# Attention by pairs of heads in a two-layer trunk on one NeuronCore: row halves for the logits, column halves for the products with V

## The chip, the core and the metric

The kernel runs on one core of a Trainium2 chip. A core has a matrix engine (TensorE, PE in the rows below, with its weight loads as PEld), a vector engine (DVE), a scalar engine (ACT), GpSimd (POOL) and SyncE (SP), which issues the loads of the weights. The metric is the time of one execution on the device in microseconds; the number given is the median of three runs.

## What is computed

A trunk of two residual layers over 256 tokens of width 1024, batch 1, float32. Each layer is attention, then a SwiGLU feed-forward of width 2816. Cut to what the change touches:

```python
# layer 0: 8 FoX heads (softmax with forget gates) and 8 stick-breaking heads, 64 wide
# layer 1: 8 MoBA heads (64 wide, bias on the logits) and 8 MLA heads (q and k 96 wide, v 64 wide)
logits = jnp.einsum("bhqd,bhkd->bhqk", qb, k) * scale     # per head, causal
p = weights_of(logits)                                    # softmax, or stick-breaking products
out = jnp.einsum("bhqk,bhkd->bhqd", p, v)                 # per head, 64 columns
x = x + concat(out of all 16 heads) @ w_out
x = x + swiglu(rms_norm(x))
```

With 256 tokens every query block sees at most two key blocks of 128, so a head has three 128 x 128 blocks of logits: one for the first 128 queries, two for the rest.

## The kernel before

Every large product (projections, output projection, feed-forward) is exact in three passes: each operand is split into two float32r parts, and `mm3` issues high by high, high by low and low by high into an accumulator `acc`. ACT makes the high part of a weight piece (`whi<-raw`), DVE the low part (`wlo<-raw,whi`). The attention itself uses plain float32 products (`mm` on float32), which the trace shows as two records each, and its tiles in PSUM are called `ps`; there are four of these.

A group is four heads; layer 0 has the groups Fox 0, Fox 1, Stick 2, Stick 3, layer 1 has Moba 0, Mla 2, Moba 1, Mla 3. For one head the steps on TensorE are:

- **Logits** (`products`, L615): two products into one `ps` tile, 128 columns for the first query block, 256 for the second. For FoX, MoBA and stick-breaking heads q and k are 64 rows: an even head lies in partitions 0 to 63, an odd one in 64 to 127 (operands `fT`, `sbT`). For MLA heads they are 96 rows (`mT`).
- DVE and ACT make the weights from them (`score`, L660 and L1065): for softmax a masked minimum on DVE (`lg`), two exponentials on ACT (`pm`), a reciprocal and two scalings on DVE.
- **Transposes** (`transp`, L624): three 128 x 128 transposes of the weights (`ident,pm` or `ident,w`), and a copy by ACT into `wt`.
- **Products with V** (`values`, L635): two products, of 256 and of 128 columns, into the group's tile `O`. The tile of V for a head is 128 columns wide, with the head's 64 columns in one half and zeros in the other (`v_zeros`, L584), so that two heads add into the same 128 partitions.

`heads_loop` (L728) writes the order by hand: the logits of head i, filler, the transposes of head i-1, filler, the products of head i-1 with V, filler. Filler are the large products that are due next (projections of later groups, parts of the output projection). How much is pulled in is told by an estimate of TensorE's time, `fl.clk`, which `mm` (L330) and `tr` advance; work of the other engines is put off with `fl.at` to a later value of that clock. The scheduler of the tile framework then moves steps marked `urgent` forward on each engine, so the final order is read from the built program and not from the loop.

Of the kernel before, what the change touches and what calls it, by code (L numbers as in the profile page):

```python
# [98 lines left out]
class Ordered:  # L99
    """An engine that keeps the order of emission while on is set, and puts nothing later before what it kept."""  # L100
# [19 lines left out]
class Weights:  # L120
    """Weights in the order of their use: loads ahead, then the exact split in two float32r parts."""
# [12 lines left out]
    def add_load(self, src, row0, total, kts, col0, ncols, beside=None):  # L134
        """beside: the load whose tile has room for this one too."""
# [11 lines left out]
    def cut(self, u, pieces):  # L147
        """pieces: (load, its rows and columns, the place of them in the unit)."""
# [15 lines left out]
    def add_first(self, src, total, col0, ncols, extra0, extra):  # L164
        """two units of half the rows, with a few more columns from another place; loads of two row tiles."""
# [90 lines left out]
def trunk_kernel(ctx: ExitStack, tc: tile.TileContext, x, ffn_norm, w_gate_up, w_down, rel_bias,  # L256
# [60 lines left out]
    def rsqrt(v, n, o=None):  # L317
        """v ** -0.5 by logarithm and exponential, with a Newton step."""
# [11 lines left out]
    def mm(o, a, b, start, stop):  # L330
# [4 lines left out]
        fl.clk += max(n / 2.4 + 2.5, 107) if b.dtype == R32 else 4 * (n / 2.4 + 1)  # L335
# [126 lines left out]
    # gains: rows of 128, transposed to columns  # L462
# [21 lines left out]
    class XT:  # L484
# [8 lines left out]
        def transposes(self, q):  # L493
            """tiles 2q and 2q+1 of the features."""
# [75 lines left out]
    def featT(src, gain):  # L570
        """[tok, 2, 256] token-major -> [128, 2 pairs, 256 tok]."""
# [12 lines left out]
    def v_zeros():  # L584
        """the tiles of V, for the two groups at hand: a head's columns are in the left or the right half."""
        res = []
        for i in range(2):
            t = att.tile([P, 2, 4, P], F32, name=nm("V"), bufs=1)
            for h in range(4):
                pool.memset(t[:, :, h, 64 - h % 2 * 64:128 - h % 2 * 64], 0.0)  # L590
            res.append(t)
        return res
# [4 lines left out]
    def v_rows(V, src, scale):  # L597
        """src: [tok, 4, 64] of the two row tiles."""
        for tok in range(2):
            for i in range(2):  # L600
                act.activation(V[:, tok, i::2, i * 64:i * 64 + 64], src[tok][:, i::2], AF.Identity,
                               scale=1.0 if scale is None else scale[:, tok:tok + 1])
        return V

    class Group:
        """four heads; score(h) gives the weights' tile, prep() brings q and k in place."""
# [28 lines left out]
        def values(self, h):  # L635
# [22 lines left out]
    class Softmax(Group):  # L658
        @urgent
        def score(self, h):  # L660
            s = self.products(h)
# [3 lines left out]
            pm = att.tile([P, 384], F32, name=nm("pm"), tag="pm")  # L665
# [5 lines left out]
            def exps():  # L671
# [3 lines left out]
                               accum_out=l[:, 1:2])  # L675

# [10 lines left out]
        def normed(self, pq, pk, rs, r2, gain):  # L687
            """q and k of a group of 64-wide heads, as their products end: squares, factors, scaled rows."""
# [39 lines left out]
    def heads_loop(groups, lead):  # L728
        """a head's scores, then the products of the head before it, filler in between."""
        n, tail = 4 * len(groups), 4500  # L730
# [3 lines left out]
        for i in range(n + 1):  # L734
            b = max(fl.total - tail - fl.used, 0) / (n - i) if i < n else tail
            if i < n:
                g, h = groups[i // 4], i % 4
# [702 lines left out]
```

## Time and profile before

| | |
|---|---|
| three runs | 635.42, 635.65, 635.81 us; median 635.65 us |
| span of the profiled execution, first to last instruction | 633.6 us |
| TensorE busy | 626.0 us, 99% |
| VectorE busy | 427.5 us, 67% |
| ScalarE busy | 339.8 us, 54% |
| attention of layer 0 | about 39 to 131 us of the span |
| feed-forward of layer 0, first projections of layer 1 | about 131 to 358 us |
| attention of layer 1 | about 358 to 433 us |
| feed-forward of layer 1 | about 433 us to the end |

The profiled execution is not one of the three timed runs, and only its span is known: the median lies 2.0 us above it, for what comes before the first and after the last instruction. A record of a product on TensorE lasts longer than the time until the next one starts, since products overlap in the array; what a product costs is therefore read from one start to the next.

### The profile page before, as it was taken

The numbers are of one execution on the slowest core, as the hardware profiler recorded it, in microseconds if no ns is written. First come the engines' busy times: TensorE is split into PE (matmuls) and PEld (weight loads), VectorE is DVE, ScalarE is ACT, GpSimd is POOL, SyncE is SP. The second block draws the span as 40 slices with busy tenths as digits, with TensorE's granted clock in tenths as the row PEclk, the third lists the DMA queues.
The fourth block names the chain that finished last, engine by engine and source line by source line (L and its number), as shares of the span: only waits on it lengthen the run. The fifth ranks groups of instructions, "written<-read, shape, count | busy, mean of one in ns | idle before, by whom it ended". The sixth has DMA issues, their size and how long they took to land.

```text
span 633.6 us, 11099 instructions
## 1 busy us (share of the span) xinstructions
PE 626.0 (99%) x4370; PEld 575.3 (91%) x4370; DVE 427.5 (67%) x915; ACT 339.8 (54%) x731; POOL 22.6 (4%) x66
## 2 busy tenths in 40 slices
PE   8999999999999999999999999999999999999997
PEld 7888998779999999988889989788999999998897
DVE  4897766666876777745556697896687677774541
ACT  6865565563544455444447585976554445454430
POOL 8300000000000000000010000000000000000000
PEclk9999999999999999999999999999999999999999
DMA  8955234446664563744556325263266456375500
GB/s 262 338 179 184 96 121 134 133 133 212 205 222 162 181 218 135 232 162 171 169 181 208 116 84 199 67 200 121 93 202 226 158 184 214 135 233 166 200 34 33
DMA packets 84212, 106.19 MB, mean 168 GB/s; under 512 B 3532, under 2 KB 69394, under 8 KB 84032
## 3 DMA queue, kind: packets, MB, share of 16 engines
q1 hardware_dynamic: 82880, 101.49, 49.5%
q0 software_dynamic: 1120, 3.86, 1.9%
q8 instruction: 34, 0.56, 0.4%
q10 hardware_dynamic: 160, 0.14, 0.1%
q14 instruction: 18, 0.15, 0.1%
HBM read 104.41 MB, written 3.17 MB: 170 GB/s over the span
## 4 chain that ended last, share of the span: by engine, by line
PE 92%; DVE 3%; DMA 2%; ACT 2%; SPq 1%; issue 0%; ACTq 0%
PE acc L113 80%; PE ps L113 11%; DVE wlo L113 1%; DMA raw<-in_ev_w_in 1%; DMA x<-in_x 1%; DVE sm L113 1%; ACT whi L113 1%; ACT V L113 0%; SPq L404 0%; SPq L205 0%; DVE qkn L113 0%; ACT fT L113 0%; DVE lg L113 0%; DVE m L113 0%; ACT sqh L113 0%
## 5 line engine op out<-in xcount | busy, mean ns | idle before, releaser
L113 DVE TENSOR_TENSOR wlo<-raw,whi 128x512 fp32r<-128x512 f32 (+3 forms) x300 | 241.5, 828 | 85.8 <-ACT whi L113 85.0
L113 ACT ACTIVATE whi<-raw 128x512 fp32r<-128x512 f32 (+3 forms) x300 | 209.3, 740 | 129.9 <-PE acc L113 117.5
L113 PE MATMUL acc<-xh,whi 128*128 128x256 f32 x768 | 218.6, 285 | 0.0
L113 PE MATMUL acc<-xh,wlo 128*128 128x256 f32 x768 | 217.4, 283 | 0.0
L113 PE MATMUL acc<-xl,whi 128*128 128x256 f32 x768 | 217.4, 283 | 0.0
L113 PEld LDWEIGHTS acc<-xh,whi 128*128 128x128 f32 x768 | 147.4, 192 | 0.4 <-issue 0.3
L113 PEld LDWEIGHTS acc<-xl,whi 128*128 128x128 f32 x768 | 147.4, 192 | 0.0
L113 PEld LDWEIGHTS acc<-xh,wlo 128*128 128x128 f32 x768 | 147.3, 192 | 0.0
L113 PE MATMUL acc<-whi,hl 128*128 128x512 f32 (+1 forms) x198 | 73.3, 370 | 0.0
L113 PE MATMUL acc<-whi,hh 128*128 128x512 f32 (+1 forms) x198 | 73.2, 370 | 0.0
L113 PE MATMUL acc<-wlo,hh 128*128 128x512 f32 (+1 forms) x198 | 73.1, 369 | 0.0
L113 PE MATMUL acc<-whi,xh 128*128 128x256 f32 (+2 forms) x240 | 71.6, 298 | 0.0
L113 PE MATMUL acc<-whi,xl 128*128 128x256 f32 (+2 forms) x240 | 69.3, 289 | 0.0
L113 PE MATMUL acc<-wlo,xh 128*128 128x256 f32 (+2 forms) x240 | 69.2, 288 | 0.0
L113 DVE TENSOR_TENSOR gs<-acc,rbc 128x512 f32<-128x512 f32 x44 | 30.4, 691 | 37.4 <-PE acc L113 37.3
L113 ACT ACTIVATE hh<-t 128x256 fp32r<-128x256 f32 x44 | 18.4, 418 | 69.4 <-DVE t L113 69.4
L113 PEld LDWEIGHTS acc<-whi,xl 128*128 128x128 f32 x240 | 45.7, 190 | 0.7 <-issue 0.7
L113 PEld LDWEIGHTS acc<-wlo,xh 128*128 128x128 f32 x240 | 45.9, 191 | 0.1
L113 PEld LDWEIGHTS acc<-whi,xh 128*128 128x128 f32 x240 | 45.8, 191 | 0.2
L113 PEld LDWEIGHTS acc<-wlo,hh 128*128 128x128 f32 x198 | 37.3, 188 | 6.7
L113 PEld LDWEIGHTS acc<-whi,hh 128*128 128x128 f32 x198 | 37.3, 188 | 6.7
L113 PEld LDWEIGHTS acc<-whi,hl 128*128 128x128 f32 x198 | 37.3, 188 | 6.7
(179 smaller groups left out, 682.1 us busy)
## 6 DMA issues: line engine op xcount, KB each, us to landing
raw<-in_ffn_w_gate_up SPq DMA_DIRECT2D x44, 1024.0 KB, 5.5
raw<-in_ffn_w_down SPq DMA_DIRECT2D x20, 1024.0 KB, 5.0
raw<-in_ev_w_in SPq DMA_DIRECT2D x10, 1024.0 KB, 8.2
raw<-in_od_w_in SPq DMA_DIRECT2D x6, 1024.0 KB, 5.5
raw<-in_ev_w_out SPq DMA_DIRECT2D x4, 1024.0 KB, 4.8
raw<-in_od_w_out SPq DMA_DIRECT2D x4, 1024.0 KB, 5.5
brep<-bd POOLq DMA_DIRECT2D x1, 2048.0 KB, 8.6
raw<-in_ffn_w_down SPq DMA_DIRECT2D x4, 512.0 KB, 3.3
```

The costliest lines, as they stand in the source:

```text
L113: r = f(*a, **k)
```

## The change

Heads are taken two at a time.

- `scores(pr)` issues the logits of an even and an odd head of 64 rows alternately: both first query blocks, then both second ones. The even head is in the upper row half of the array, the odd head in the lower. For MLA, whose heads have 96 rows, the order is the same, with no halves.
- `values(pr)` uses V tiles of 64 columns without zeros. The even head writes partitions 0 to 63 of `O`, the odd head 64 to 127, so their products lie in the two column halves of the array; they alternate too. `v_tiles` takes the place of `v_zeros`, and `v_rows` needs one ACT instruction for each row tile where it had two.
- `heads_loop` goes by pairs: 8 steps for four groups where it had 16, with two heads' transposes together, other shares of filler, and a longer reserve at the end (`tail`). Flags "e" keep a pair's logits behind the exponentials of the pair before.
- The tiles `pm` and `m` get four buffers, and FoX makes two masks ahead.
- The clock of `mm` counts 120 ns at least for a float32r product (107 before) and half the time for products that are meant to lie beside each other.

```diff
-    def mm(o, a, b, start, stop):
+    def mm(o, a, b, start, stop, beside=1):
...
-        fl.clk += max(n / 2.4 + 2.5, 107) if b.dtype == R32 else 4 * (n / 2.4 + 1)
+        fl.clk += max(n / 2.4 + 15, 120) if b.dtype == R32 else 4 * (n / 2.4 + 1) / beside
...
-            t = att.tile([P, 2, 4, P], F32, name=nm("V"), bufs=1)
...
+        return [att.tile([P, 2, 4, 64], F32, name=nm("V"), bufs=1) for _ in range(2)]
...
-            for i in range(2):
-                act.activation(V[:, tok, i::2, i * 64:i * 64 + 64], src[tok][:, i::2], AF.Identity,
-                               scale=1.0 if scale is None else scale[:, tok:tok + 1])
+            act.activation(V[:, tok], src[tok], AF.Identity, scale=1.0 if scale is None else scale[:, tok:tok + 1])
...
-        def products(self, h):
-            qT, kT = self.heads[h]
-            s = ps()
-            mm(s[:, 0:P], qT[:, 0:P], kT[:, 0:P], True, True)
-            mm(s[:, P:384], qT[:, P:256], kT, True, True)
-            return s
+        def scores(self, pr):
+            two = [(self.heads[2 * pr + i], ps()) for i in range(2)]
+            n = 2 if self.heads[0][0].shape[0] == 64 else 1
+            for (qT, kT), s in two:
+                mm(s[:, 0:P], qT[:, 0:P], kT[:, 0:P], True, True, n)
+            for (qT, kT), s in two:
+                mm(s[:, P:384], qT[:, P:256], kT, True, True, n)
+            for i, (_, s) in enumerate(two):
+                self.score(2 * pr + i, s)
...
-            wt = self.wt[h]
-            o = self.O[:, h // 2 * 256:h // 2 * 256 + 256]
-            mm(o, self.V[:, 0, h], wt[:, 0:256], h == 0, False)
-            mm(o[:, P:256], self.V[:, 1, h], wt[:, 256:384], False, h == 3)
+            o = self.O[:, pr * 256:pr * 256 + 256]
+            for b in range(2):
+                for i in range(2):
+                    wt = self.wt[2 * pr + i][:, b * 256:384 - (1 - b) * P]
+                    mm(o[64 * i:64 * i + 64, b * P:256], self.V[:, b, 2 * pr + i], wt, b == 0, b == 1, 2)
...
-        n, tail = 4 * len(groups), 4500
+        n, tail = 2 * len(groups), 6000
...
+                if i > 0:
+                    g.ready(pr, "e")
+                g, pr = groups[i // 2], i % 2
+                g.scores(pr)
+            fl.pull((0.35 if i < n else 0.6) * b)
...
+                for j in range(2):
+                    g1.transp(2 * pr1 + j)
```

On TensorE in layer 0, first group, third head, the program before reads as follows: the logits of the third head (`ps_791`) stand between the two products of the first head with V (`ps_780`), with float32r products (`acc`) on both sides.

```order
L113 MATMUL acc_691<-wlo_479,xh_257 128x256
L113 MATMUL acc_691<-whi_478,xl_261 128x256
L113 MATMUL ps_780<-wt_761,V_353 128x256
L113 MATMUL ps_791<-fT_644,fT_637 128x128
L113 MATMUL ps_791<-fT_644,fT_637 128x256
L113 MATMUL ps_780<-wt_761,V_353 128x128
L113 MATMUL acc_691<-wlo_479,xh_263 128x256
```

The program of the change at its first products with V, again on TensorE (`ps_929` is the group's `O`, `ps_960` and `ps_961` are the logits of the next pair):

```order
L113 MATMUL acc_922<-xl_187,whi_707 128x256
L113 MATMUL acc_922<-xh_179,wlo_708 128x256
L113 MATMUL ps_929<-wt_846,V_353 64x256
L113 MATMUL ps_929<-wt_852,V_353 64x256
L113 MATMUL ps_929<-wt_846,V_353 64x128
L113 MATMUL ps_929<-wt_852,V_353 64x128
L113 MATMUL ps_960<-fT_904,fT_897 128x128
L113 MATMUL ps_961<-fT_904,fT_897 128x128
L113 MATMUL ps_960<-fT_904,fT_897 128x256
L113 MATMUL ps_961<-fT_904,fT_897 128x256
L113 MATMUL acc_922<-xh_189,whi_707 128x256
```

Where one head's two products stood, four products of two heads stand, 64 partitions of output each; the pair's logits follow in one block. In the whole program the logits of 64 rows stand in 22 places before (20 with one head, 2 with two) and in 10 after (8 with one pair, 2 with two pairs one behind the other), the products with V in 32 and in 16.

The second place is TensorE at the end of layer 1's attention: the last head's transposes (`ps_5257`), its products with V (`ps_5168`), and the output projection. Before:

```order
L113 MATMUL ps_5257<-ident,pm_5218 128x128 x3
L113 MATMUL acc_4957<-whi_4970,oh_5128 128x512
L113 MATMUL acc_4957<-wlo_4971,oh_5128 128x512
L113 MATMUL acc_4957<-whi_4970,ol_5132 128x512
L113 MATMUL ps_5168<-wt_5261,V_3861 128x256
L113 MATMUL ps_5168<-wt_5261,V_3861 128x128
L113 MATMUL acc_4956<-whi_4970,oh_5130 128x512
```

And in the change, where `pm_5135` and `pm_5142` are the last two heads and `ps_5167` is their `O`:

```order
L113 MATMUL ps_5198<-ident,pm_5135 128x128 x2
L113 MATMUL ps_5204<-ident,pm_5142 128x128 x3
L113 MATMUL acc_4949<-whi_4969,ol_5115 128x512
L113 MATMUL ps_5167<-wt_5202,V_3841 64x256
L113 MATMUL ps_5167<-wt_5208,V_3841 64x256
L113 MATMUL ps_5167<-wt_5202,V_3841 64x128
L113 MATMUL ps_5167<-wt_5208,V_3841 64x128
L113 MATMUL acc_4950<-whi_4969,oh_5111 128x512
```

Between the last transposes and the products that need their copies stood three products of 512 columns; now one stands there. The pair before the last has the same row of steps.

## Rows read from the trace of the kernel before

**Rows 1.** The page: busy time of each engine, share of the span, instructions.

```profile
PE 626.0 (99%) x4370; PEld 575.3 (91%) x4370; DVE 427.5 (67%) x915; ACT 339.8 (54%) x731; POOL 22.6 (4%) x66
```

**Rows 2.** The page: the chain that ended last, share of the span by engine.

```profile
PE 92%; DVE 3%; DMA 2%; ACT 2%; SPq 1%; issue 0%; ACTq 0%
```

**Rows 3.** TensorE's groups by shape: operands, count | busy us, mean ns.

```profile
L113 PE MATMUL ps<-wt,V 128*128 128x256 f32 x64 | 19.8, 390 | 0.0
...
L113 PE MATMUL ps<-fT,fT 64*128 64x256 f32 x32 | 8.4, 377 | 0.0
...
L113 PE MATMUL ps<-sbT,sbT 64*128 64x256 f32 x16 | 4.8, 377 | 0.0
```

**Rows 4.** Timeline of TensorE (start, duration, records): logits among transposes, transposes alone.

```profile
62.10 0.27 PE L113 MATMUL ps<-ident,pm 128*128 128x128 f32 x1
62.30 0.92 PE L113 MATMUL ps<-fT,fT 64*128 64x128 f32 x4
63.15 0.44 PE L113 MATMUL ps<-ident,pm 128*128 128x128 f32 x2
...
63.55 0.28 PE L113 MATMUL acc<-xl,whi 128*128 128x256 f32 x1
...
68.38 0.49 PE L113 MATMUL ps<-ident,pm 128*128 128x128 f32 x3
...
68.83 0.28 PE L113 MATMUL acc<-xl,whi 128*128 128x256 f32 x1
```

**Rows 5.** Timeline of TensorE: logits of two heads, one behind the other.

```profile
38.73 0.28 PE L113 MATMUL acc<-wlo,xh 128*128 128x256 f32 x1
38.93 0.93 PE L113 MATMUL ps<-fT,fT 64*128 64x128 f32 x8
39.80 0.38 PE L113 MATMUL acc<-whi,xl 128*128 128x256 f32 x1
40.02 0.28 PE L113 MATMUL acc<-whi,xh 128*128 128x256 f32 x1
```

**Rows 6.** Timeline of TensorE: one head's products with V between filler.

```profile
64.73 0.28 PE L113 MATMUL acc<-xh,wlo 128*128 128x256 f32 x1
64.85 0.81 PE L113 MATMUL ps<-wt,V 128*128 128x256 f32 x4
...
65.62 0.28 PE L113 MATMUL acc<-xl,whi 128*128 128x256 f32 x1
```

**Rows 7.** Timeline of TensorE: transposes with 8 columns of output (forget gates).

```profile
27.67 0.38 PE L113 MATMUL ps<-ident,fg 128*8 128x128 f32 x2 [1.24 <-DVE sm L113]
27.81 0.37 PE L113 MATMUL acc<-whi,xh 128*128 128x256 f32 x1
28.01 0.28 PE L113 MATMUL acc<-wlo,xh 128*128 128x256 f32 x1
```

**Rows 8.** Timeline of weight loads: the first behind rows 7, and behind rows 5.

```profile
27.78 0.19 PEld L113 LDWEIGHTS acc<-whi,xh 128*128 128x128 f32 x1
...
39.80 0.19 PEld L113 LDWEIGHTS acc<-whi,xl 128*128 128x128 f32 x1 [0.33 <-issue]
```

**Rows 9.** Windows: stretch, its length, busy us of each engine, clock, DMA share, GB/s.

```profile
39.00:58.00 19.00, 18.77 (x143) 16.65 (x142) 16.21 (x62) 12.21 (x38) 0.00 (x0) 1.00 0.50 162
...
358.00:433.00 75.00, 74.80 (x471) 63.36 (x471) 60.70 (x213) 56.39 (x165) 0.00 (x0) 1.00 0.35 117
```

**Rows 10.** ACT's groups by shape in 360 to 440 us: the copy of transposed weights.

```profile
L113 ACT ACTIVATE wt<-ps 128x384 f32<-128x384 f32 x16 | 7.9, 492 | 9.3 <-PE ps L113 9.3
```

**Rows 11.** Timeline of TensorE at the end of layer 1's attention: last transposes, last V.

```profile
430.94 0.49 PE L113 MATMUL ps<-ident,pm 128*128 128x128 f32 x3
431.18 0.48 PE L113 MATMUL acc<-whi,oh 128*128 128x512 f32 x1
...
432.07 0.92 PE L113 MATMUL ps<-wt,V 128*128 128x256 f32 x4
```

More of the change, by code (lines that the diff above doesn't have):

```diff
@@ L582, in featT, with v_tiles @@
         return t
-    def v_zeros():
-        res = []
-        for i in range(2):
-            t = att.tile([P, 2, 4, P], F32, name=nm("V"), bufs=1)
[L589 to L592, printed above, removed]
+    def v_tiles():
+        return [att.tile([P, 2, 4, 64], F32, name=nm("V"), bufs=1) for _ in range(2)]
     def heads_of(a):
@@ L599, in v_rows @@
         for tok in range(2):
-            for i in range(2):
-                act.activation(V[:, tok, i::2, i * 64:i * 64 + 64], src[tok][:, i::2], AF.Identity,
-                               scale=1.0 if scale is None else scale[:, tok:tok + 1])
+            act.activation(V[:, tok], src[tok], AF.Identity, scale=1.0 if scale is None else scale[:, tok:tok + 1])
         return V
@@ L614, in products, with ready @@
         @urgent
-        def products(self, h):
-            qT, kT = self.heads[h]
-            s = ps()
-            mm(s[:, 0:P], qT[:, 0:P], kT[:, 0:P], True, True)
-            mm(s[:, P:384], qT[:, P:256], kT, True, True)
-            return s
+        def scores(self, pr):
[7 more added lines that the diff above has]
+                self.score(2 * pr + i, s)
+        def ready(self, pr, what):
+            for i in range(2):
+                fl.need((what, self, 2 * pr + i))
         @pinned
@@ L634, in values @@
         @urgent
-        def values(self, h):
+        def values(self, pr):
             if self.O is None:
                 self.O = ps()
-            wt = self.wt[h]
-            o = self.O[:, h // 2 * 256:h // 2 * 256 + 256]
-            mm(o, self.V[:, 0, h], wt[:, 0:256], h == 0, False)
-            mm(o[:, P:256], self.V[:, 1, h], wt[:, 256:384], False, h == 3)
+            o = self.O[:, pr * 256:pr * 256 + 256]
+            for b in range(2):
+                for i in range(2):
+                    wt = self.wt[2 * pr + i][:, b * 256:384 - (1 - b) * P]
+                    mm(o[64 * i:64 * i + 64, b * P:256], self.V[:, b, 2 * pr + i], wt, b == 0, b == 1, 2)
         @urgent
@@ L659, in score @@
         @urgent
-        def score(self, h):
-            s = self.products(h)
+        def score(self, h, s):
             m0, m1 = self.mask(h)
@@ L664, in score @@
             lg = att.tile([P, 384], F32, name=nm("lg"), tag="lg")
[L665 removed]
+            pm = att.tile([P, 384], F32, name=nm("pm"), tag="pm", bufs=4)
             mx = sm(2)
@@ L675, in exps @@
                                accum_out=l[:, 1:2])
+                fl.flags.add(("e", self, h))
             @urgent
@@ L736, in heads_loop @@
             if i < n:
-                g, h = groups[i // 4], i % 4
-                g.score(h)
-            fl.pull((0.45 if i < n else 0.5) * b)
-            if i > 0:
-                g1, h1 = groups[(i - 1) // 4], (i - 1) % 4
-                fl.need(("w", g1, h1))
-                g1.transp(h1)
-            if i < n and h == 3 and i + 1 < n:
-                groups[i // 4 + 1].prep()
-            fl.pull((0.5 if i < n else 0.15) * b)
+                if i > 0:
[3 more added lines that the diff above has]
+            fl.pull((0.35 if i < n else 0.6) * b)
+            if i > 0:
+                g1, pr1 = groups[(i - 1) // 2], (i - 1) % 2
+                g1.ready(pr1, "w")
+                for j in range(2):
+                    g1.transp(2 * pr1 + j)
+            if i < n and pr == 1 and i + 1 < n:
+                groups[i // 2 + 1].prep()
+            fl.pull((0.35 if i < n else 0.15) * b)
             if i > 0:
@@ L749, in heads_loop @@
                     fl.need(("V", g1))
-                g1.values(h1)
-                if h1 == 3:
+                g1.values(pr1)
+                if pr1 == 1:
                     g1.outputs()
-            fl.pull((0.2 if i < n else 0.35) * b)
+            fl.pull((0.35 if i < n else 0.25) * b)
     xn = {}
@@ L957, in trunk_kernel @@
     OT = [None] * KT
-    vz = v_zeros()
+    vz = v_tiles()
     cd = dram.tile([4, 256], F32, name="cd")
@@ L1035, in prep, with score @@
             self.masks(0)
-        def score(self, h):
-            super().score(h)
-            if h < 3:
-                fl.at(1500, lambda: self.masks(h + 1))
+            self.masks(1)
+        def score(self, h, s):
+            super().score(h, s)
+            if h < 2:
+                fl.at(1500, lambda: self.masks(h + 2))
     class Stick(Group):
@@ L1064, in score @@
         @urgent
-        def score(self, h):
-            s = self.products(h)
+        def score(self, h, s):
             z = att.tile([P, 384], F32, name=nm("z"), tag="lg")
-            be = att.tile([P, 384], F32, name=nm("be"), tag="m")
+            be = att.tile([P, 384], F32, name=nm("be"), tag="m", bufs=4)
             cp = att.tile([P, 3, 129], F32, name=nm("cp"), tag="cp")
-            w_ = att.tile([P, 384], F32, name=nm("w"), tag="pm")
+            w_ = att.tile([P, 384], F32, name=nm("w"), tag="pm", bufs=4)
             kp = keep[h % 2]
@@ L1079, in sig @@
                 act.activation(be, z, AF.Sigmoid, scale=0.125)
+                fl.flags.add(("e", self, h))
             @urgent
@@ L1173, in trunk_kernel @@
     att = att_pool.__enter__()
-    vz = v_zeros()
+    vz = v_tiles()
     mob = att.tile([P, 8, 256], F32, name="mob", bufs=1)
```

2 lines of the change are left out of this document (1 added, 1 removed).

## The prediction

> **What bounds the kernel now.** I read the page's busy table first: TensorE is busy 626.0 of the 633.6 us of the span, the next engine, DVE, 427.5 [rows 1]. The chain that ended last says the same: 92% of it runs over TensorE, no other engine has more than 3% [rows 2]. So the time is, to a few us, the sum of the steps between TensorE's starts, and a change is worth what it takes out of that sum, less the waits that it opens. DVE and ACT matter only where TensorE would run out of other products; in the attention of layer 1 DVE is closest to that, 60.7 us busy of 75 [rows 9].
>
> The groups by shape tell how much attention there is: 32 + 16 records of 256 columns with 64 rows (two records a product), so 24 heads of 64 rows, and 64 records of 256 columns with V, so 32 heads [rows 3].
>
> **Logits: what a place with them costs.** From the first transpose of one head to the second product of filler behind it pass 63.55 - 62.10 = 1.45 us with another head's logits in between; the same transposes without logits take 68.83 - 68.38 = 0.45 us [rows 4]. One head's logits cost TensorE 1.00 us. Their own columns are only part of it. The products with V have the same columns and cost 65.62 - 64.73 = 0.89 us less two steps of filler, 0.24 (0.12 each, from 64.73 to 64.85): 0.65 us [rows 6]. The other 0.35 us of a logits place is paid for going into the 64-row form of the array and out of it.
>
> Two heads in one place already occur, and they are the best evidence of all: eight records start at 38.93, and filler begins again at 39.80 [rows 5]. From 38.73 to 40.02 are 1.29 us, less 0.24 of filler 1.05 us for two heads. So the two row halves work side by side in this very program, in float32, and the second head costs 0.05 us. The built program had them one head after the other there, so issuing alternately is not what brings the overlap; standing together is.
>
> Before, 20 heads stand alone and 4 stand in twos: 20 x 1.00 + 2 x 1.05 = 22.1 us. After, there are 12 pairs, 12 x 1.05 = 12.6, and in two places two pairs follow each other, which saves one change of form each, 2 x 0.35: 11.9 us. **Saved: 10.2 us.** The MLA heads have 96 rows, take the whole array, and are left at nothing.
>
> **Products with V.** Before: 32 x 0.65 = 20.8 us [rows 6]. After: 16 places with the same columns as one head, if the column halves work side by side. No row shows two products in two column halves, so I bound the cost of one place. Below: full overlap and no price for the change of form, 0.65 us, as one head now. Above: no overlap, and the price of the row form, 1.30 + 0.35 = 1.65 us. The sum over 16 places lies between 10.4 us (10.4 saved) and 26.4 (5.6 lost).
>
> On the change of form there is one near row: the transposes of the forget gates have 8 columns of output and so use a part of the columns. Their two records and the filler step behind take 28.01 - 27.67 = 0.34 us [rows 7], and full-width transposes take the same: three and a filler step 0.45, so 0.11 each and 0.12 [rows 4]. The next weights are loaded at 27.78, before the product that uses them at 27.81, so ahead of the array as usual; behind the row form the load at 39.80 has waited 0.33 us [rows 7, 8]. So the way out of a narrow column form was free here, and I take no price for it. The way in is hidden behind a wait there and stays open.
>
> The Trainium skill, page "TensorEngine Tiling (Array Packing)", section Key Properties, states that a change of the tiling mode drains the array. The trace agrees for row halves, with 0.35 us a place, and not for the way out of the 8-column form. By that rule the products with V would cost 16 x 0.35 = 5.6 us more; that is the first rival below.
>
> On the overlap I take the row halves as the nearest row: 1.05 us for what alone costs 2.00 [rows 4, 5], so the second head is nearly free. **Saved: 10.4 us, with 0.65 us a place.**
>
> **What the change opens.** With pairs, two copies of transposed weights stand between the transposes and the products with V, 0.49 us each, one after the other on ACT [rows 10]. Nearly everywhere filler covers them. At the end of layer 1 it gets thin: now three products of 512 columns, 432.07 - 431.18 = 0.89 us, cover one copy [rows 11]; after, one product, about 0.3 us, covers two. The first copy starts under the second head's transposes (0.33 us). The second ends about 0.98 us and a hand-over of 0.1 after the first head's transposes, and TensorE has 0.33 + 0.3 to do: a wait of about 0.45 us, in each of the last two pairs, 0.9. At the start of layer 1's attention two heads' exponentials must end before the first transposes where one head's did; I give 0.5 us. For DVE, whose load stays and whose stage gets shorter, 0.6 us more. **Lost: 2.0 us.** If the cover is gone everywhere, 16 places x 0.45 = 7.2 us.
>
> Small edits: one ACT instruction for V in place of two, no zeros on POOL, which is busy 22.6 us in all [rows 1]: nothing, for neither engine is waited for there. The higher estimate of a float32r product moves `fl.at` work earlier by some products everywhere; TensorE is never short of products in the feed-forwards, so nothing. In the prologue the forget gates' transposes come ten products earlier, before their data, so their wait of 1.24 us [rows 7] grows, but the products behind are only moved: nothing, bounded by 1.2 us.
>
> **The sum.** 633.6 - 10.2 - 10.4 + 2.0 = 615.0 us of span, and the 2.0 us around it: **617.0 us** against a median of 635.65.
>
> **The rivals.**
> - *The column form is paid like the row form.* For it: 0.35 us in each place of the row form [rows 4]; against it: the free way out in rows 7. 617.0 + 5.6 = 622.6 us.
> - *The column halves don't overlap*, so half of the change doesn't do what it says: two streams through all 128 rows at once are shown by no row. Each place costs 1.30 us, the saving of 10.4 is gone: 627.4 us. The Trainium skill, page "TensorE: Matmul & The Clock Gate", section Measured speedup vs the span model, gives 2.38 times for three column tiles; an estimate of 1.6 times for two would put a place at 0.81 us and the sum at 619.6. No run here shows it.
> - *DVE becomes the bound of layer 1's attention.* Its 75 us lose 3.2 us of logits (six heads alone and one place with two become four pairs) and 5.2 of V, so some 67 remain for DVE's 60.7. The densest stretch now has DVE at 16.2 of 19.0 us, 85%, with TensorE still busy [rows 9]. If 85% is the limit, the stage needs 71.4 us: about 4 us lost, 621.
> - *Slower: each change between the halves costs like a change of form.* Alternating the halves makes three such changes in a place beside the way in and out: 0.35 / 2 x 3 + 0.35 = 0.88 us on top of 1.30, without overlap. 16 x 0.88 = 14.1 more than before, less 10.2, plus 2.0: 641.5 us. It decides from (10.2 - 2.0) / 16 = 0.51 us above 1.30 a place. Against it: the row halves run side by side at no such price [rows 5].
>
> **How the numbers follow.** Forecast 0.52; column form paid 0.14; no overlap 0.14; DVE bound 0.12; slower 0.04; another 0.04 for a better outcome than forecast, or one near the old time. The range goes from 614.0 (a wait of 2 us less, and a logits saving of 11) to 627.6, the case without overlap; left out are the slower case and combinations of rivals. About 0.2%, 1.3 us, is what a measurement of this kernel can tell from no change; faster by more 0.94, within 0.02, slower by more 0.04.
>
> **What the changed profile would show.** Step one: ten places with logits of 64 rows, eight with 8 records in about 0.87 us and two with 16; if each pair takes 1.7 us it is wrong. Step two: places with eight records of V of 64 columns; starts in twos and about 0.65 us from the first to the filler mean overlap; 1.3 us means none. A weight load behind them that starts ahead of its product means that the form is free, a gap of 0.2 to 0.4 us that it is paid. Step three: TensorE's waits on ACT `wt` at the end of layer 1, about 1 us in all. Wrong as a whole if TensorE is busy for under 95% of the span, or if the feed-forwards have changed length.

## The result and the profile after

The changed kernel takes 626.5 us (626.2 to 626.6) where the kernel before takes 635.6 (635.4 to 635.8): a ratio of 0.9853 with a 95% interval of 0.9839 to 0.9867, 9.1 us less. The forecast was 617.0 with a range of 614.0 to 627.6. The time lies in the range and on the right side, but only half of the forecast gain of 18.6 us came. It is near the time of one rival (no overlap of the column halves, 627.4), and this rival is one that the trace refutes.

The page of the changed kernel, TensorE's busy time and the chain that ended last, to be read beside [rows 1, 2]:

```profile
PE 612.3 (98%) x4370; PEld 563.2 (90%) x4370; DVE 424.6 (68%) x915; ACT 336.1 (54%) x715; POOL 20.4 (3%) x50
...
PE 89%; DVE 5%; ACT 3%; DMA 2%; SPq 1%; issue 0%; ACTq 0%; DVEq 0%
```

TensorE is busy 13.7 us less, the span is only 9.2 shorter (624.4 after 633.6): 4.5 us of the gain came back as time in which TensorE waits, 3.0 of them in the attention of layer 1 and 1.1 in the first 45 us. The chain shows it too: DVE and ACT now hold 8% of it, 5% before.

**The products with V, between filler.** TensorE's timeline (start, duration, records) of the changed kernel, the answer to [rows 6]:

```profile
64.68 0.28 PE L113 MATMUL acc<-xl,whi 128*128 128x256 f32 x1
64.80 0.28 PE L113 MATMUL acc<-xh,wlo 128*128 128x256 f32 x1
65.01 0.87 PE L113 MATMUL ps<-wt,V 128*64 128x256 f32 x8
65.81 0.39 PE L113 MATMUL acc<-xh,whi 128*128 128x256 f32 x1
66.03 0.28 PE L113 MATMUL acc<-xl,whi 128*128 128x256 f32 x1
```

Two heads' eight records take 65.81 - 65.01 = 0.80 us, so the two column halves do work side by side; one after the other they would be 2 x 0.65 = 1.30 [rows 6]. From the last filler product ahead to the second one behind are 66.03 - 64.80 = 1.23 us, less two steps of 0.12: a place costs 0.99 us, not 0.65. To see where the other 0.34 us go, one line of the kernel before is needed, the first filler product behind the one head of [rows 6]:

```profile
65.42 0.36 PE L113 MATMUL acc<-xh,whi 128*128 128x256 f32 x1
```

Its step to the next filler product, 65.62 - 65.42 = 0.20 us, is as long as the 0.22 behind the column halves, so that step alone is no sign of a price. The way in is one: 65.01 - 64.80 = 0.21 us, where it was 0.12, so 0.09 is paid there. The way out is the larger part. In the records themselves the last product with V and the second filler product behind it are 0.42 us apart, and 0.23 in the kernel before: 0.19 paid. The remaining 0.06 lie inside the place.

The weight loads in the same place show it, as [rows 8] did for the row form:

```profile
65.01 0.63 PEld L113 LDWEIGHTS ps<-wt,V 128*64 128x64 f32 x8
65.81 0.19 PEld L113 LDWEIGHTS acc<-xh,whi 128*128 128x128 f32 x1 [0.17 <-issue]
65.92 0.19 PEld L113 LDWEIGHTS acc<-xl,whi 128*128 128x128 f32 x1
```

The filler's weights are loaded at 65.81, with its product and not ahead of it, and the load has waited 0.17 us. Behind the 8-column transposes of [rows 7] no load waits like that [rows 8].

**The logits, well placed and badly placed.** TensorE's timeline of the changed kernel at 72 us (V and logits beside each other) and at 78 us (logits right behind transposes):

```profile
71.69 0.87 PE L113 MATMUL ps<-wt,V 128*64 128x256 f32 x8
72.49 0.93 PE L113 MATMUL ps<-sbT,sbT 64*128 64x128 f32 x8
73.34 0.38 PE L113 MATMUL acc<-whi,xh 128*128 128x256 f32 x1
...
77.75 0.82 PE L113 MATMUL ps<-ident,pm 128*128 128x128 f32 x6
78.50 1.64 PE L113 MATMUL ps<-sbT,sbT 64*128 64x128 f32 x8
80.08 0.39 PE L113 MATMUL acc<-xh,whi 128*128 128x256 f32 x1
```

At 72.49 a pair takes 0.85 us, as forecast. At 78.50 the same eight records take 1.58. The weight loads there (`sbT` is q and k of the stick-breaking heads) say why:

```profile
78.50 0.52 PEld L113 LDWEIGHTS ps<-sbT,sbT 64*128 64x128 f32 x4 [0.17 <-DVE w L113]
79.22 0.52 PEld L113 LDWEIGHTS ps<-sbT,sbT 64*128 64x128 f32 x4 [0.21 <-ACT wt L113]
```

The second head's four loads wait for ACT's copy `wt`. The kernel has four `ps` tiles; `O`, the two heads' transposes and the two heads' logits want five, so the second head's logits wait until the copy has freed one, and by then, in this place, the first head's are done: nothing is left to lie beside.

**The wait in layer 1.** What TensorE waited for from 352 to 424 us, with the number of times and the longest; for the kernel before, from 355 to 433 us, the same answer is empty:

```profile
PE acc L113 <- ACT whi L113: 2.9, 2, 1.9
```

and the windows around the longer of the two (stretch, length, busy us of TensorE, of its weight loads, of DVE, ACT and POOL, granted clock, DMA share, GB/s):

```profile
391.62:393.72 2.10, 0.15 (x1) 0.00 (x0) 1.61 (x7) 2.10 (x7) 0.00 (x0) 1.00 0.00 0
393.72:396.89 3.17, 3.17 (x7) 2.29 (x8) 3.17 (x7) 3.17 (x7) 0.00 (x0) 0.51 0.00 0
396.89:400.00 3.11, 3.11 (x14) 2.58 (x13) 3.11 (x8) 3.11 (x8) 0.00 (x0) 0.95 0.60 178
```

In these 2.1 us no product begins, and TensorE stands still for 1.95 of them, waiting for the split of the out projection's weights, while ACT is busy without a break: it has the softmax of a pair, the copies of MLA's rows and the split to do at once. Behind it TensorE's clock is granted at 0.51, the lower level of 1.2 GHz, for 3.2 us, in which seven products of 512 columns begin instead of some fourteen: another 1.6 us. So ACT, not DVE, was the engine that ran short there. The lower clock does not follow such a pause each time; experiment 4 has the same pause without it.

### The profile page after: what moved, and what is told of

Read it like the earlier page. It is cut to its first block, busy times and chain, and to the rows that moved or that the text cites. A ratio compares the mean times of both kernels' runs of the same rounds, so it can differ in the third digit from the quotient of the medians.

```text
span 624.4 us, 11053 instructions
## 1 busy us (share of the span) xinstructions
PE 612.3 (98%) x4370; PEld 563.2 (90%) x4370; DVE 424.6 (68%) x915; ACT 336.1 (54%) x715; POOL 20.4 (3%) x50
## 4 chain that ended last, share of the span: by engine, by line
PE 89%; DVE 5%; ACT 3%; DMA 2%; SPq 1%; issue 0%; ACTq 0%; DVEq 0%
PE acc L113 81%; PE ps L113 8%; DVE wlo L113 2%; DMA raw<-in_ev_w_in 1%; DVE sm L113 1%; ACT whi L113 1%; DMA x<-in_x 1%; DVE m L113 1%; ACT pm L113 1%; SPq L405 0%; ACT sqh L113 0%; ACT V L113 0%; DVE lg L113 0%; DVE qkn L113 0%; SPq L205 0%
## 5 line engine op out<-in xcount | busy, mean ns | idle before, releaser
L113 DVE TENSOR_TENSOR wlo<-raw,whi 128x512 fp32r<-128x512 f32 (+4 forms) x300 | 240.7, 827 | 83.6 <-ACT whi L113 83.1
(178 smaller groups left out, 627.8 us busy)
```

Source lines behind the costliest of these rows:

```text
L113: r = f(*a, **k)
```

## The experiments

The theory going in: the column form is paid per place (about 5 us of the missing 9.5), ACT's bunched work in layer 1 costs some 4, and the shortage of `ps` tiles some 1.4. The rivals stand with each run. Times are medians; the kernel before stood at 635.3 to 635.9 beside them, so a difference between two runs is good to about 0.5 us.

**1. What each half of the change is worth.** First the changed kernel with V back in full width:

```diff
+t = att.tile([P, 2, 2, 192], F32, name=nm("V"), bufs=1)
+pool.memset(t[:, :, :, 64:128], 0.0)
...
-for b in range(2):
-    for i in range(2):
-        wt = self.wt[2 * pr + i][:, b * 256:384 - (1 - b) * P]
-        mm(o[64 * i:64 * i + 64, b * P:256], self.V[:, b, 2 * pr + i], wt, b == 0, b == 1, 2)
+for i in range(2):
+    h = 2 * pr + i
+    wt, v = self.wt[h], self.V[:, :, pr, 64 * i:64 * i + 128]
+    mm(o, v[:, 0], wt[:, 0:256], h == 0, False)
+    mm(o[:, P:256], v[:, 1], wt[:, 256:384], False, h == 3)
```

> The changed kernel with only its products with V put back: each head has its columns of V beside zeros in a full-width operand, two products a head, head after head, in the same 16 places of two heads; the logits stay as changed. (Two temporaries of the rotation have one buffer instead of two, to make room for the zeros.) My theory: the column form overlaps two heads but is paid per place, on the way in and out: a place of two heads takes 0.99 us in the changed kernel's trace (65.0 us) against 2 x 0.65 = 1.30 in the full-width form, so 16 x 0.31 = 5.0 slower than the changed kernel's 626.5: 631.5 us. Rival, the price eats the whole gain: 626.5, no change. Rival, no price, as I forecast, the loss being elsewhere: 16 x 0.65 = 10.4 slower, 636.9.

Measured: 629.25 us (ratio to before 0.9884 to 0.9917), 2.7 more than the changed kernel and not 5.0. TensorE's busy time rose by 5.4 (617.7 after 612.3), about as the theory has it, but it stood idle for 1.9 us less, 1.3 of these in the first 45 us. The clock differs as well: two executions took 629.8 and 629.9 us, with 0.997 granted over the span as in the changed kernel, and two 628.2 and 628.7, with 1.000. The windows of this run at its wait for ACT, behind it, and at 27.7 us:

```profile
397.20:399.10 1.90, 0.21 (x2) 0.01 (x1) 1.57 (x7) 1.90 (x9) 0.00 (x0) 1.00 0.00 0
399.10:402.00 2.90, 2.90 (x11) 2.04 (x12) 2.90 (x6) 2.87 (x6) 0.00 (x0) 1.00 0.00 0
...
27.68:31.09 3.41, 3.41 (x18) 3.16 (x17) 2.71 (x10) 1.12 (x4) 0.54 (x1) 0.50 1.09 348
```

Here the clock stays at 1.00 behind the wait for ACT, and the lower level comes behind another wait, that of the forget gates' transposes. The run mixes the price of V with that of the waits and is no clean measure of either; it was made again without the wait for ACT, after experiment 3 had shown how, with the old estimate of a product's time beside the same edit:

> The changed kernel with both the full-width V (zeros beside each head's columns, head after head) and the old estimate: what is left of the change is the logits in pairs. With it the time with everything but the new estimate (622.7) splits into its two halves without the waits that the new estimate opens. My theory: 16 places of V at 1.30 instead of 0.99 us, 5.0 more than 622.7: 627.7 us, so that the logits in pairs are worth 635.5 - 627.7 = 7.8 and V 5.0. Rival, the waits ate more of V's gain than the trace shows, and the column form is worth 8 to 10: 631 to 633. Rival, it is worth nothing: 622 to 623.5.

Measured: 627.58 us (0.9851 to 0.9884). With the 622.7 of experiment 3 the change has three parts: the logits in pairs, with the loop over pairs that goes with them, 635.6 to 627.6, 8.0 us; V in column halves 627.6 to 622.7, 4.9 us; and the new estimate, 3.8 us lost again. Measured each against the kernel before beside it (635.9 here, 635.3 in experiment 3), the first two are 8.3 and 4.3.

**2. Is it the alternation?** Both places issued head after head, in the halves as changed:

```diff
 for (qT, kT), s in two:
     mm(s[:, 0:P], qT[:, 0:P], kT[:, 0:P], True, True, n)
-for (qT, kT), s in two:
     mm(s[:, P:384], qT[:, P:256], kT, True, True, n)
...
-for b in range(2):
-    for i in range(2):
+for i in range(2):
+    for b in range(2):
```

> The changed kernel with the products of a pair issued head after head in both the logits and the products with V, still in the halves of the array and still in the same places: only the alternation is gone. My theory: TensorE starts in order and overlaps only neighbours in different halves, so of the four products of a place only the second and the third run side by side: about 0.21 + 0.43 + 0.43 = 1.07 us instead of 0.65 for the logits and 0.43 + 0.43 + 0.21 = 1.07 instead of 0.65 for V. 16 places of V x 0.42 = 6.7, and 7 of the 8 places of 64-row logits that overlap x 0.42 = 2.9: 636 us, all of the gain. Rival, nothing overlaps without alternation: 16 x 0.65 + 7 x 0.65 = 15 slower, 641. Rival, standing together in a place is what counts and the queue overlaps by itself: 626.5.

Measured: 626.51 us, the same as the changed kernel (626.5); my theory failed, the last rival held. TensorE's timeline of this run at the place shown above:

```profile
64.85 0.28 PE L113 MATMUL acc<-xh,wlo 128*128 128x256 f32 x1
65.06 0.88 PE L113 MATMUL ps<-wt,V 128*64 128x256 f32 x8
65.87 0.39 PE L113 MATMUL acc<-xh,whi 128*128 128x256 f32 x1
```

Eight records in 0.81 us again. In the records themselves the four of 256 columns begin before the first of 128, in twos 0.01 us apart. A head has one product of 256 columns, and it leaves two records, so two of the four are the second head's: its first product begins 0.01 us behind the first head's, and ahead of the first head's second product, which stands before it in the built program. Standing in one place is what brings the overlap; the order inside does nothing.

**3. The estimate of a product's time.** The forecast had put the edit of the planner's clock at nothing. Undone in the changed kernel, and done alone in the kernel before (there without `beside`, since that kernel has no pairs):

```diff
-fl.clk += max(n / 2.4 + 15, 120) if b.dtype == R32 else 4 * (n / 2.4 + 1) / beside
+fl.clk += max(n / 2.4 + 2.5, 107) if b.dtype == R32 else 4 * (n / 2.4 + 1)
```

> The changed kernel with the old estimate of a product's time in the planner's clock (n / 2.4 + 2.5, at least 107, and no halving for products side by side). My theory: the estimate only decides how much filler stands between two steps, and the gain is in TensorE's products: within 1 us of 626.5. Rival, the slower running clock of the old estimate puts about a tenth more filler between the steps, and the waits of layer 1 (2.1 us at 391.4, 1.1 at 355.4) shrink: 623 to 625. Rival, the new estimate carries part of the gain: 628 to 631.

> The kernel before with only the new estimate of a product's time (n / 2.4 + 15, at least 120). My theory: within 1 us of the kernel before, 634.6 to 636.6, since its TensorE hardly waits. Rival, the estimate is part of the gain: 632 to 634. Rival, it costs waits, which the changed kernel pays too: 637 to 639.

Measured: 622.72 us for the changed kernel with the old estimate (0.9788 to 0.9817), 3.8 less; 639.01 for the kernel before with the new one (1.0045 to 1.0075), 3.7 more. Two kernels, the same price: the estimate costs 3.7 us by itself. That the sizes agree is partly chance, for the waits are not the same ones. In the kernel before with the new estimate TensorE waited, from 355 to 440 us, mostly for the copies at the end of the attention, with the clock at 1.000:

```profile
PE ps L113 <- ACT wt L113: 1.3, 1, 1.3
PE acc L113 <- ACT oh L113: 0.5, 1, 0.5
PE ps L113 <- DVE sm L113: 0.3, 1, 0.3
```

All that TensorE waited for from 352 to 424 us in the changed kernel with the old estimate:

```profile
PE ps L113 <- DVE pm L113: 0.3, 1, 0.3
PE ps L113 <- DVE qn L113: 0.2, 1, 0.2
```

Both waits for `whi` are gone, and with them the slow clock (1.000 over the span). Why does a truer estimate do harm? The loops over heads divide a total of filler, `12 * 5235` and `6 * 5235 + 2 * 3300`, that is written in the old estimate's ns. The next run gives them the new one's:

```diff
-fl.start(fill0(), 12 * 5235)
+fl.start(fill0(), 9 * 5840 + 3 * 5480)
...
-fl.start(fill1(), 6 * 5235 + 2 * 3300)
+fl.start(fill1(), 3 * 5840 + 3 * 5480 + 2 * 3470)
```

> The changed kernel with its new estimate kept, and only the two totals of the filler that the loops over heads divide brought to the new estimate's units: 9 x 5840 + 3 x 5480 in place of 12 x 5235 for layer 0, 3 x 5840 + 3 x 5480 + 2 x 3470 in place of 6 x 5235 + 2 x 3300 for layer 1. It asks why the old estimate gave 622.7 where the new one gives 626.5. My theory: with the new estimate the totals are a tenth too small, so the pairs of heads are strung too close and ACT's work of layer 1 falls on one another (2.1 us of wait at 391.4 and 1.1 at 355.4): with fitting totals these go and the time is 622 to 623.5. Rival, the work that is due after so many ns of the planner's clock comes too early by the new estimate, whatever the totals: 626 to 627. If half of each: 624 to 625.

Measured: 623.95 us (0.9799 to 0.9835): 2.6 of the 3.8 us come back, so the stale totals are most of it: with them the steps of the loop share a tenth less filler in layer 0 and 7% less in layer 1, and ACT's work falls closer together. One wait for `whi`, of 1.1 us, remains. The rest may lie in the steps that are due after so many ns of the planner's clock; that was not tried apart.

**4. Can the wait for ACT be cured by the order of ACT's queue?** First with the split of the weights 2.0 blocks of weights ahead of its use, where it was 1.8:

```diff
-AHEAD = 1.8
+AHEAD = 2.0
```

> The changed kernel with the split of the weights issued 2.0 units ahead of their use instead of 1.8. It asks whether the wait of 2.1 us at 391.4, for ACT's part of the out projection's weights, and the clock of 0.73 behind it come from that instruction being late in ACT's queue. My theory: ACT is full there (6.0 of 6.0 us), so an order a little earlier gains its 0.2 units, about 1 us of the wait and part of the slow stretch: 624 to 625.5. Rival, ACT's load is all that counts: 626.5. Rival, earlier splits push the softmax's own steps back, which the transposes wait for: 627 to 629.

Measured: 626.6 us, no change beyond the scatter of its four executions (625.4 to 628.1), and TensorE's wait is as long as it was. ACT's order around it had stayed the same, so the run tells nothing about the order. It tells something about the clock. The windows of the wait and behind it, in an execution of 625.4 us:

```profile
392.14:394.09 1.95, 0.00 (x1) 0.01 (x1) 1.46 (x6) 1.95 (x7) 0.00 (x0) 1.00 0.00 0
394.09:397.30 3.21, 3.07 (x12) 2.26 (x13) 3.21 (x8) 3.21 (x7) 0.00 (x0) 1.00 0.00 0
```

The same pause as in the changed kernel, and the clock stays at 1.00. The two fastest executions have 0.999 granted over the span, the two slowest (627.8 and 628.1) 0.995 and 0.994. The next run does change ACT's order, giving the split the softmax's priority in layer 1's attention:

```diff
-self.act.activation(hi, src, AF.Copy)
+if self.boost:
+    with self.act.tc.high_priority(offset=400):
+        self.act.activation(hi, src, AF.Copy)
+else:
+    self.act.activation(hi, src, AF.Copy)
...
+W.boost = True
 heads_loop([moba[0], mla[0], moba[1], mla[1]], 2500)
+W.boost = False
```

> The changed kernel, with its new estimate, where ACT's split of the weights has the same priority as the softmax's steps during the attention of layer 1 (elsewhere as it was). Splitting 2.0 units ahead had left ACT's order around the wait at 391.4 as it was; here the order changes: the out projection's splits stand ahead of the copies of MLA's rows. My theory: the wait of 2.1 us and the 1.6 us of the slow clock behind it come from that order: both go, 622.5 to 624. Rival, ACT's load is what counts, and the wait only moves to the softmax's steps or the transposes: 625.5 to 627.5. Rival, it gets worse since the steps that are pushed back are longer: 628 or more.

Measured: 632.15 us (0.9924 to 0.9959), 5.6 slower: my theory failed, the last rival held. What TensorE waited for from 394 to 403 us in this run:

```profile
PEld acc L113 <- ACT qn L113: 6.5, 2, 6.1
PE acc L113 <- ACT qn L113: 5.7, 1, 5.7
```

and what ACT did in that time (timeline: start, duration, records):

```profile
394.20 2.18 ACT L113 ACTIVATE whi<-raw 128x512 fp32r<-128x512 f32 x4
396.28 0.63 ACT L113 ACTIVATE oh<-ps 128x256 fp32r<-128x256 f32 x2
396.81 4.26 ACT L113 ACTIVATE whi<-raw 128x512 fp32r<-128x512 f32 x8
400.96 0.47 ACT L113 ACTIVATE qn<-acc 128x384 f32<-128x384 f32 x1
```

Now eight splits, 4.26 us, stand ahead of the copy `qn`, and that copy is what frees the accumulators that the out projection needs. In both orders TensorE waits, for whichever work of ACT goes last, which speaks for ACT's load in these microseconds; the old estimate, with more filler between the pairs (experiment 3), takes the wait away. An order between the two, with only the first splits ahead of the copies, was not tried. Part of the 5.6 us is the clock: over the profiled execution, the slowest of the four, 0.989 was granted.

**5. The price of the column form: of what?** The transposes of the forget gates, which had shown no price at 8 columns [rows 7], widened to 64 and to 32 (on the kernel of experiment 7):

```diff
+lf = att.tile([P, 2, 64], F32, name="fg5", bufs=1)
+pool.memset(lf, 0.0)
...
-tr(p_[:8, tok * P:tok * P + P], lf[:, tok], ident)
+tr(p_[:64, tok * P:tok * P + P], lf[:, tok], ident)
```

> The kernel with all four heads' V in one place and the old estimate (616.7), with the two transposes of the forget gates widened from 8 to 64 columns of output (the other 56 hold zeros that nobody reads). It asks why the way out of those transposes was free while that of V's 64 columns costs 0.10 us. My theory: the width decides; with 64 columns the filler behind the transposes comes about 0.1 us later: some 0.20 us from the second transpose to the first filler and a first filler step of 0.22 instead of 0.12, 0.2 in all. Rival, the position decides (V's second head sits in the right half, the gates in the left alone): no change there, 0.11 and 0.12. The time itself stays within 0.5 us of 616.7 in both.

> The same with 32 columns instead of 64. If the width decides, this tells on which side 32 columns lie: by what the 8 columns showed I expect the free way out, 0.11 and 0.12 us; a price like that of 64 columns (0.20 and 0.22) would put the bound between 8 and 32. The time within 0.5 us of 616.7.

Measured: 616.75 and 616.61 us, one run each, against 616.67. TensorE's timeline with 64 columns:

```profile
27.12 0.38 PE L113 MATMUL ps<-ident,fg 128*64 128x128 f32 x2 [0.79 <-DVE sm L113]
27.25 0.36 PE L113 MATMUL acc<-whi,xh 128*128 128x256 f32 x1
27.45 0.28 PE L113 MATMUL acc<-wlo,xh 128*128 128x256 f32 x1
```

From 27.12 to 27.45 are 0.33 us, as with 8 columns (0.34), and with 32 columns it is the same (26.85 to 27.19). The expectation looked at the first filler step, 0.22 against 0.12, and that was the wrong pair: the step is 0.20 here, and 0.20 behind full-width products too. The fair measure is from the last record to the second filler product: 0.23 us here with 64 columns, 0.23 behind full-width products with V, 0.42 behind V's column halves. So the width does not decide; the rival held. The same 64 columns cost 0.19 us on the way out where a second stream runs in the right half, and nothing where the left half works alone. Two things more differ: these are transposes, which leave one record each, and V's are float32 products with two; and the way in is hidden behind the wait for DVE. Whether the right half, the two streams or the kind of product makes the price stays open. For the row halves no second stream is needed: one head alone pays 0.35 us [rows 4], in either half.

**6. The shortage of `ps` tiles.** With the old estimate, the logits held behind the products emitted so far:

```diff
+@pinned
 @urgent
 def scores(self, pr):
```

> The changed kernel with the old estimate (622.7), with the logits held behind the products emitted so far, so that the scheduler doesn't pull them up behind the transposes of the pair before. My theory: in four places (61.4, 81.3, 102.3 and 387.5 of the trace with the old estimate) the second head's tile in PSUM comes free only after ACT's copy, and the pair overlaps not or in part: 1.23, 1.54, 1.29 and 1.39 us where 0.87 is to be had. Held back, all pairs take 0.87: 2.0 us saved; but the two places with two pairs of logits are torn apart (2 x 0.35 lost) and some three changes of form that V and logits share (0.2 each): 622.0, 0.7 less than with the old estimate; in the trace every place of 64-row logits at 0.87. Rival, the second head's lateness has another cause: the places stay at 1.2 to 1.5 and the time rises to 624.

Measured: 621.77 us, 0.95 less than with the old estimate (0.7 was expected). TensorE's timeline of one of the four places, here at 77.42, which takes 1.54 us at 81.35 with the old estimate alone:

```profile
77.21 0.28 PE L113 MATMUL acc<-xh,wlo 128*128 128x256 f32 x1
77.42 0.93 PE L113 MATMUL ps<-sbT,sbT 64*128 64x128 f32 x8
78.27 0.38 PE L113 MATMUL acc<-xh,whi 128*128 128x256 f32 x1
```

0.85 us, and 0.85 to 0.87 in all twelve places. That the bad places come from logits pulled up behind transposes is shown; that it is for want of a `ps` tile is read from the loads' wait for `wt`, and a fifth tile was not tried. Nearly half of the gain is given back: logits that stood beside V or beside another pair now need their own way in and out, and the steps of V's products sum to 14.3 us, 13.0 with the old estimate alone.

**7. Fewer places.** With the old estimate, V of all four heads of a group in one place:

```diff
-g1.values(pr1)
 if pr1 == 1:
+    g1.values(0)
+    g1.values(1)
     g1.outputs()
...
-wt = att.tile([P, 384], F32, name=nm("wt"), tag="wt")
+wt = att.tile([P, 384], F32, name=nm("wt"), tag="wt", bufs=4)
...
```

> The changed kernel with the old estimate (622.7), and the products with V of all four heads of a group in one place behind the second pair's transposes, eight places in place of 16; four tiles for the transposed weights instead of two (two small temporaries give up their second buffer for that). My theory: the column form is paid per place, 0.34 us whatever stands in it, so eight places less save 2.7; besides, the places where a pair's logits stood right behind transposes, and overlapped only in part for want of a tile in PSUM, are fewer, 1 us at most; and three or four shared changes of form between products with V and logits are lost, 0.2 each: 618.5 to 620.5. Rival, the price is per product, not per place: 622 to 623, no change. Rival, eight copies and products at the end of layer 1 open a new wait of 1 to 2 us: 621 to 622.

Measured: 616.67 us (616.2 to 617.1), ratio to before 0.9702 (0.9687 to 0.9717): 6.0 us less than with the old estimate, more than I expected, and 9.8 less than the changed kernel. TensorE's timeline of one such place, followed by the next pair's logits:

```profile
61.73 0.28 PE L113 MATMUL acc<-xh,wlo 128*128 128x256 f32 x1
61.94 1.52 PE L113 MATMUL ps<-wt,V 128*64 128x256 f32 x16
63.39 0.93 PE L113 MATMUL ps<-fT,fT 64*128 64x128 f32 x8
64.24 0.39 PE L113 MATMUL acc<-xh,whi 128*128 128x256 f32 x1
```

Sixteen records in 1.45 us, against twice 0.80, and one way in and out instead of two: the 0.34 us per place are saved as forecast, 2.7 us over eight places. The rest is on TensorE's other steps: no pair of logits stands behind transposes any more, every pair that stands alone takes 0.85 to 0.87 (2.1 us), and the steps of the 96 transposes in layer 1's attention sum to 8.6 us instead of 10.0; why these got shorter was not tried apart.

## Why the prediction was half right

**Logits: right in mechanism, 2.2 us too much.** Forecast 10.2 saved, measured 8.0. The price of the row form and the overlap were as read from [rows 4, 5]: 0.85 to 0.87 us a pair. What failed is that all twelve pairs would get it. The sum took the pairs from the code and did not ask whether two logits tiles are free at the time; behind a pair's transposes they are not, and three or four places take 1.2 to 1.9 us. In the run that gives the 8.0 (the second of experiment 1) three pairs take 1.24, 1.43 and 1.86 us and a fourth falls apart into two places of 0.85: together 2.8 us more than 0.86 each, where 2.2 are missing. There the second head of the longest waits like this (weight loads):

```profile
83.20 0.52 PEld L113 LDWEIGHTS ps<-sbT,sbT 64*128 64x128 f32 x4 [0.49 <-ACT wt L113]
```

Experiment 6 gives all places 0.87 us and takes 1.7 us out of TensorE's steps in them.

**Products with V: the step that failed is "I take no price for it".** Forecast 10.4 saved at 0.65 us a place, measured 4.9, at 0.99. The overlap is there (0.80 us for two heads). I had a row for the form in each of two directions: the row form, 0.35 us paid, and the 8-column transposes, nothing paid, and took the second because it was about columns. Experiment 5 shows that it was not an instance of the thing: narrow transposes alone in the left half leave at no price, with 8, 32 or 64 columns. (The split of [rows 4, 7] into 0.11 us a transpose and 0.12 a filler step has the sum right and the parts wrong: the first filler product begins 0.03 us behind the last transpose, and its step is 0.20. The conclusion on the way out stands.) The first rival (the column form paid like the row form, 1.00 us a place, 5.6 us) had the right size; the chances gave it 0.14. The Trainium skill, page "TensorEngine Tiling (Array Packing)", section Key Properties, says that a change of the tiling mode drains the array. The trace agrees for V's places (0.34 us each) and not for the narrow transposes.

**Waits: the step that failed is the estimate, put at "nothing".** I looked for its effect in the feed-forwards, where there is none, and not in the two loops that divide a total written in the old unit. It costs 3.7 us in either kernel (experiment 3); 2.0 had been put down for waits at other places. Of those the tail of layer 1 was about right. TensorE's timeline and its weight loads at the last place but one with V:

```profile
420.24 1.25 PE L113 MATMUL ps<-wt,V 128*64 128x256 f32 x8
421.42 0.33 PE L113 MATMUL ps<-ident,pm 128*128 128x128 f32 x1
...
420.24 0.19 PEld L113 LDWEIGHTS ps<-wt,V 128*64 128x64 f32 x2 [0.33 <-ACT wt L113]
420.62 0.62 PEld L113 LDWEIGHTS ps<-wt,V 128*64 128x64 f32 x6 [0.19 <-ACT wt L113]
```

The place takes 421.42 - 420.24 = 1.18 us instead of 0.80, since the second head's loads wait for its copy, and it starts some 0.1 late; the last place is the same. That is about 0.5 us each where 0.45 was put down. With the old estimate these two places take 0.95 and 0.80, so these waits, too, hang mostly on the filler.

Together 617.0 + 2.2 + 5.5 + 1.8 = 626.5 us. That the three terms make up the whole miss proves nothing by itself, since they are differences along one chain of four times and must add up; what carries them are the places' own steps: 0.34 us in each of V's 16 places, 2.8 us in the badly placed logits, and the waits for ACT with the clock behind them. That the time came out near the rival of 627.4 is chance.

**The other rivals.** No overlap: refuted by the 0.80 us. DVE as the bound of layer 1: near in size only, and the wrong engine; in the window of the wait ACT is busy 2.10 of 2.10 us and DVE 1.61, and with the old estimate the stage has no such wait. A price for each change between the halves: refuted by the 0.80 us inside a place, where it put 1.30 and more; alternating or not makes no difference either.

## What to carry to other kernels

Count changes of form, not products: a visit of V's products to the two column halves costs 0.34 us here, with 8 records in it or with 16, so work in the halves belongs together in few places. The version with half as many places is 9.8 us faster than the changed kernel; 3.8 of that is the estimate undone and 6.0 the places and what follows from them. Before a gain is counted per pair, count the tiles that a pair needs at the moment it is to run. And when a planner's unit of time is corrected, every constant written in that unit is part of the change.

## What was not expected of the hardware

- Products in different halves begin together even where they are queued head after head: the second head's first product starts 0.01 us behind the first head's and ahead of a product that stands before it. The Trainium skill, page "TensorE: Matmul & The Clock Gate", section "The mechanism", says that products start strictly in the queue's order; the records of experiment 2 differ.
- Transposes with 8, 32 or 64 columns alone in the left half leave at no price (0.33 to 0.34 us for two of them and a filler step; 0.23 us from the last record to the second filler product, as behind full-width products), while two streams of 64 columns side by side need 0.42 there.
- A pause of about 2 us brought the lower clock in some places and not in others. Behind 1.95 us without products the changed kernel was granted 1.2 GHz (0.51) for 3.2 us; behind 1.95 us in the first run of experiment 4 it kept 2.4 GHz (1.00). In the first run of experiment 1 it kept 1.00 behind 1.7 us of waiting for ACT, and was granted 0.50 from 27.7 us on, soon after a wait of 2.1 us; a wait of 2.0 us in the same place of the changed kernel kept 1.00. The length of the pause alone does not decide it here; what else does, no run shows.
